# Attention outputs of two heads issued in turn, projections one step ahead and outputs one step behind, in a two-block transformer kernel

## The chip, the cores and the metric

The kernel runs on one core of a Trainium2 chip. The metric is the device time of one execution in microseconds (us), the median of several runs. The profile is one further execution, recorded instruction by instruction.

## The reference, cut to what matters

256 tokens of width 1024 pass through two blocks. The first mixes differential attention, an RWKV recurrence and attention over a memory, and ends in a mixture of 16 experts. The second holds four feed-forward layers, with a mixer after the first (`hybrid_ab_mixer`) and one after the third (`swa_sink_mixer`). What the change touches are the three attentions with heads of 64 columns:

```python
# memory attention: 4 heads of 64
s = jnp.einsum('bshd,bmhd->bhsm', q, mk) * (MEM_HEAD_DIM ** -0.5)
o = jnp.einsum('bhsm,bmhd->bshd', jax.nn.softmax(s, axis=-1), mv)
...
# hybrid mixer: heads A (8 of 64) with a banded, dilated causal bias
o_a = dilated_mixture(qa, ka, va, table[:, :A_HEADS])
# heads B (8 of 64): each query keeps the 64 keys with the best index score
sc = jax.nn.relu(jnp.einsum('bqhd,bsd->bqhs', qib, k_idx))
score = jnp.einsum('bqhs,bqh->bqs', sc, wb) * idx_scale
_, idx = lax.top_k(score, topk)                  # topk = 64
o_b = dsa_attention(qb, kb, vb, q_idx, k_idx, w_idx, table[:, A_HEADS:], topk)
...
# sliding-window mixer: 16 heads of 64, 2 key heads, sinks
o, lse = banded_attention(q, k, v, bias, C_WINDOW - 1)
o = o * jax.nn.sigmoid(lse - sinks)[..., None]
```

## The kernel before, in words

All weights stream from memory in 2 MB pieces (`load`, L91, issued by SyncE). Each piece is cut into slices of 128x1024, and each slice into a high part (`wh`, a copy on ScalarE, L99) and a low part (`wl`, a subtraction on VectorE, L100). A product with weights is three TensorE products (`mm3`, L105 to L107). A framework gives every engine its instruction list: it runs a simulated timeline when the kernel is built and at each point takes, of the instructions that it believes to be ready, the one that the code names first. So the code's order is a priority, and the list that results is fixed: on the chip each engine works through it in that order.

The hybrid mixer (`hyb`) and the sliding-window mixer (`swa`) go over 8 steps, each of two heads (128 columns). A step projects q (and k) for its two heads (`projT`, 24 products of 128x128 by 256 columns each), takes them out of PSUM with one VectorE instruction (`evac_rows`, L386), makes the scores (`attn_scores`, L295 and L296 on TensorE, then bias, maximum, exponential and division on VectorE and ScalarE, L301 to L312), transposes the weights (L325), copies them to SBUF (`pT`, L327) and multiplies with v (L329, L330). The last two products exist once for each head `e` of the pair and write 64 partitions of one PSUM bank, `po[64*e:64*e+64]`; they use 64 columns of the array. ScalarE and VectorE take the bank out as a high and a low part (L331, L332). fp32 products appear as two records each in the trace.

`staggered` runs the steps: `first(j+1)` (projection and scores) is named ahead of `second(j)` (transposes, copies and products with v, in `attn_out`); after the last `first` the first part of the output projection (`project_back`) is named. For each head `attn_out` names transposes, copy and both products before it turns to the next head.

In `hyb` the heads B need an additive mask `madd`. `index()`, called at step 2, makes it: 6 small projections, 8 pairs of score products (L492, L494), 16 VectorE instructions that add them up (L500), and then for each of two query blocks 8 rounds of `max` and `match_replace` (L507, L509), which strike out the 64 best keys. Steps 4 to 7 add the mask to their bias on GpSimd (L538).

`mem_attn` in the first block does the same as `attn_out` over two steps with 256 keys (L1095 transposes, L1098 copies, L1101 products). `diff_attn` and the expert layer use `staggered` too, with their own `first` and `second`.

Of the kernel before, what the change touches and what calls it, by code (L numbers as in the profile page):

```python
# [11 lines left out]
F32 = mybir.dt.float32  # L12
# [4 lines left out]
OP = mybir.AluOpType  # L17
# [4 lines left out]
T = 256  # L22
# [4 lines left out]
class Net:  # L27
# [364 lines left out]
    def swa(self, h, x, follow):  # L392
        W = self.I["swa"]
        xh, xl, rs = x
        kv = self.projN(self.by_k(self.load(self.I["swa_kv"]), 256), 0, 256, xh, xl, True)
        v = self.natural([ps[:, 128:] for ps in kv], self.pair(128, "vs0", "vs1"), rs)
        kT = [self.repeated_T([ps[:, 64 * g:64 * g + 64] for ps in kv], rs, "kT", 2) for g in range(2)]
        bc = self.row_bc(rs)
        oh, ol = self.o_tiles()
        raws, bias = {}, {}  # L400

        def first(j):
            g, c = divmod(j, 4)
            if j % 2 == 0:
                bias[0] = self.load_bias(16 + 2 * j)
            if c == 0:
                raws[g] = self.load(W[g])
            qT = self.evac_rows(self.projT(self.by_col(raws[g], c), xh, xl), bc, 0.125, "qT", 2)
            return self.attn_scores(qT, kT[g], [self.head_bias(bias[0], 2 * (j % 2) + e) for e in range(2)],
                                    self.col("sinks", 2 * j, 2))  # L410

        x, after = follow()
        self.staggered(8, first, lambda j, s2: self.attn_out(s2, v, [64 * (j // 4)] * 2, oh, ol, j),
                       self.project_back([W[2], W[3]], oh, ol, h, range(8), TAIL["swa"], after))
        return x

    def natural(self, ps, out, rs):
# [21 lines left out]
    def hyb(self, h, x, follow):  # L439
        nc, wk = self.nc, self.ph  # L440
        W = self.I["hyb"]
# [31 lines left out]
        def index():  # L473
# [14 lines left out]
            for hd in range(8):  # L488
# [10 lines left out]
                for b, sl, cz in blocks:  # L499
                    nc.vector.scalar_tensor_tensor(new[:, sl], rl[:, sl], cw[b][:, 256 + hd:257 + hd],  # L500
                                                   cz if score is None else score[:, sl], OP.mult, OP.add)
                score = new
            for b, sl, _ in blocks:
                cur = score
                for it in range(8):
                    m8 = wk.tile([128, 8], F32, name=self.nm("m8"), tag="m8", bufs=2)
                    nc.vector.max(m8, cur[:, sl])  # L507
                    nxt = wk.tile([128, 384], F32, name=self.nm("rep"), tag="score", bufs=3)
                    nc.vector.match_replace(nxt[:, sl], m8, cur[:, sl], -3.0e38)  # L509
                    cur = nxt  # L510
                nc.vector.tensor_scalar(madd[:, sl], cur[:, sl], -2.0e38, -1.0e30, OP.is_gt, OP.mult)

        oh, ol = self.o_tiles()
        raws, bias = {}, {}

        def first(j):
# [4 lines left out]
            c = 2 * (j % 2)  # L521
            hb = [self.head_bias(bias[0], c + e) for e in range(2)]
            if j < 4:
                if j % 2 == 0:
                    raws[0] = self.load(W[1 + j // 2])
                qT = self.evac_rows(self.projT(self.by_col(raws[0], c), xh, xl), bc, 0.125, "qa", 2)
                kT = self.evac_rows(self.projT(self.by_col(raws[0], c + 1), xh, xl), bc, 1.0, "ka", 2)
                return self.attn_scores(qT, kT, hb)
# [4 lines left out]
            kT = self.evac_rows(self.projT(self.by_col(raws[0], j - 4), xh, xl), bc, 1.0, "ka", 2)  # L533
# [6 lines left out]
            return self.attn_scores(qb[j - 4], kT, bb)  # L540

        def second(j, s2):
            c = 128 * (j % 4)
            self.attn_out(s2, v[j // 4], [c, c + 64], oh, ol, j)

        x, after = follow()
        self.staggered(8, first, second,
                       self.project_back([W[5], W[6]], oh, ol, h, range(8), TAIL["hyb"], after))
        return x

    def mixers(self, x, more, follow):
# [512 lines left out]
    def mem_attn(self, qT, kT, mkv, oh, ol):  # L1064
# [22 lines left out]

        def second(j, s2):
            po = self.acc()
            for e in range(2):  # L1090
                r = slice(64 * e, 64 * e + 64)
# [5 lines left out]
                pT = sb([512], "mpT", 2)  # L1097
                nc.scalar.copy(pT, pt)  # L1098
                c = 256 + 128 * j + 64 * e
                for kb in range(2):  # L1100
                    nc.tensor.matmul(po[r, :T], mkv[kb][:, c:c + 64], pT[:, kb * 256:kb * 256 + 256],  # L1101
                                     start=kb == 0, stop=kb == 1)
# [591 lines left out]
```

## Time and profile before

| what | before |
|---|---|
| runs | 1427.21, 1427.64, 1431.28 us; median 1427.64 |
| profiled execution | 1430.63 us, its span 1428.9 us |
| TensorE clock granted, mean over the span | 0.979 |
| TensorE products busy | 1378.0 us (96%) |
| VectorE busy | 747.7 us (52%) |
| ScalarE busy | 610.0 us (43%) |
| HBM read | 291.45 MB |

The span runs from the first to the last instruction of the profiled execution; the rest of its own time, 1.7 us, lies around it. Busy times of TensorE are modelled, and overlapping records are counted once, so distances from one start to the next say more than durations. In the views PE is TensorE, PEld its weight loads, DVE VectorE, ACT ScalarE, POOL GpSimd, SP SyncE. Times are us from the start of the span.

### The profile page before, as it was taken

How to read it: one execution, taken by the hardware profiler on the slowest of the kernel's cores; microseconds unless marked ns; L12 is line 12 of the kernel's file. 1: busy time of each engine (PE TensorE's matmuls, PEld its weight loads, DVE VectorE, ACT ScalarE, POOL GpSimd, SP SyncE). 2: the span in 40 equal slices, each digit the busy share in tenths (PEclk: the TensorE clock that was granted, in tenths of full speed). 3: DMA queues.
4: the chain of work that ended last, by engine and by line, in shares of the span. 5: the costliest groups of instructions: out<-in, count | busy, mean ns of one | idle time of the engine just before them, and what ended most of it. 6: DMA issues, size and time to landing. Idle time of an engine off the chain costs nothing.

```text
span 1428.9 us, 18895 instructions
## 1 busy us (share of the span) xinstructions
PE 1378.0 (96%) x7650; PEld 1051.2 (74%) x7650; DVE 747.7 (52%) x1250; ACT 610.0 (43%) x961; POOL 77.5 (5%) x123
## 2 busy tenths in 40 slices
PE   8999989998998999999999999999999989999997
PEld 7787664343336888888777888878888877788886
DVE  6867641121116655457865655455554567555543
ACT  5545421011113544347454544345444366545442
POOL 1133100000000000000110000000000000000001
PEclk9999889999998999999999999999999999999999
DMA  7262489999956555446334555445553642464420
GB/s 315 93 230 91 185 327 414 409 424 428 422 216 236 183 191 184 153 171 251 115 106 147 184 191 183 178 178 188 189 205 125 241 158 75 139 229 177 177 89 30
DMA packets 35370, 293.81 MB, mean 206 GB/s; under 512 B 3728, under 2 KB 8112, under 8 KB 16080
## 3 DMA queue, kind: packets, MB, share of 16 engines
q1 hardware_dynamic: 29952, 286.58, 53.1%
q10 hardware_dynamic: 5328, 5.98, 1.3%
q8 instruction: 62, 1.02, 0.3%
q14 instruction: 28, 0.23, 0.0%
HBM read 291.45 MB, written 1.10 MB: 205 GB/s over the span
## 4 chain that ended last, share of the span: by engine, by line
PE 65%; DVE 3%; ACT 1%; issue 1%; ACTq 0%; POOLq 0%; POOL 0%
PE acc L105 20%; PE acc L107 20%; PE acc L106 20%; PE tr L213 1%; PE acc L329 1%; DVE wl L100 1%; PE tr L325 1%; PE acc L296 1%; PE acc L295 1%; PE acc L330 0%; ACT sq L119 0%; DVE h L376 0%; DVE h L378 0%; DVE xf L139 0%; ACT wh L99 0%
## 5 line engine op out<-in xcount | busy, mean ns | idle before, releaser
L100 DVE TENSOR_TENSOR wl<-raw,wh 128x1024 fp32r<-128x1024 f32 (+1 forms) x349 | 426.1, 1224 | 377.0 <-ACT wh L99 374.9
L99 ACT CAST wh<-raw 128x1024 fp32r<-128x1024 f32 (+1 forms) x349 | 364.6, 1048 | 408.6 <-PE acc L107 358.1
L105 PE MATMUL acc<-wh,xh 128*128 128x512 f32 (+1 forms) x896 | 334.5, 375 | 2.4 <-ACT xh L140 1.8
L107 PE MATMUL acc<-wh,xl 128*128 128x512 f32 (+2 forms) x896 | 333.2, 373 | 1.7 <-DVE xl L141 1.5
L106 PE MATMUL acc<-wl,xh 128*128 128x512 f32 (+1 forms) x896 | 333.1, 372 | 0.0
L105 PEld LDWEIGHTS acc<-wh,xh 128*128 128x128 f32 x896 | 170.4, 190 | 32.2 <-ACT xh L140 3.0
L107 PEld LDWEIGHTS acc<-wh,xl 128*128 128x128 f32 x896 | 170.3, 190 | 31.7 <-DVE xl L141 3.7
L106 PEld LDWEIGHTS acc<-wl,xh 128*128 128x128 f32 x896 | 170.5, 190 | 28.3 <-DVE lent L732 0.6
L107 PE MATMUL acc<-wh,hl 128*128 128x512 f32 x352 | 137.5, 391 | 0.0
L106 PE MATMUL acc<-wl,hh 128*128 128x512 f32 x352 | 137.1, 389 | 0.0
L105 PE MATMUL acc<-wh,hh 128*128 128x512 f32 x352 | 137.0, 389 | 0.0
L106 PEld LDWEIGHTS acc<-wl,hh 128*128 128x128 f32 x352 | 66.1, 188 | 13.8
L105 PEld LDWEIGHTS acc<-wh,hh 128*128 128x128 f32 x352 | 66.1, 188 | 13.5
L107 PEld LDWEIGHTS acc<-wh,hl 128*128 128x128 f32 x352 | 66.1, 188 | 13.4
L105 PE MATMUL acc<-xh,wh 128*128 128x256 f32 x224 | 67.6, 302 | 1.2 <-ACT wh L99 0.6
L106 PE MATMUL acc<-xl,wh 128*128 128x256 f32 x224 | 65.6, 293 | 0.6 <-DVE xl L141 0.6
L107 PE MATMUL acc<-xh,wl 128*128 128x256 f32 x224 | 65.7, 295 | 0.0
L111 POOL TENSOR_SCALAR rstd<-ss 128x1 f32<-128x1 f32 x22 | 9.3, 422 | 965.8 <-ACT sq L119 964.3
L1303 PE MATMUL acc<-half,xe 128*64 128x512 f32 x248 | 59.6, 596 | 0.0
L1336 DVE TENSOR_SCALAR yf<-tr,gate 128x512 f32<-128x512 f32 x16 | 12.0, 751 | 81.0 <-PE tr L1329 80.8
L105 PEld LDWEIGHTS acc<-xh,wh 128*128 128x128 f32 x224 | 45.2, 202 | 5.0 <-issue 2.4
L106 PEld LDWEIGHTS acc<-xl,wh 128*128 128x128 f32 x224 | 45.1, 201 | 1.1 <-DVE xl L141 0.9
(454 smaller groups left out, 1681.5 us busy)
## 6 DMA issues: line engine op xcount, KB each, us to landing
raw<-in_ffn SPq DMA_DIRECT2D x63, 2048.0 KB, 8.0
half<-in_moe SPq DMA_DIRECT2D x45, 1024.0 KB, 12.9
raw<-in_moe SPq DMA_DIRECT2D x13, 2048.0 KB, 16.0
raw<-in_hyb SPq DMA_DIRECT2D x7, 2048.0 KB, 8.2
wl<-in_moe SPq DMA_DIRECT2D x23, 512.0 KB, 13.4
wh<-in_moe SPq DMA_DIRECT2D x23, 512.0 KB, 14.4
raw<-in_win SPq DMA_DIRECT2D x4, 2048.0 KB, 10.7
raw<-in_swa SPq DMA_DIRECT2D x4, 2048.0 KB, 9.2
```

What stands on the lines that cost most here:

```text
L99: nc.scalar.copy(hi[:, :n], x)
L100: nc.vector.tensor_tensor(lo[:, :n], x, hi[:, :n].bitcast(F32), OP.subtract)
L105: mm(out, a[0], b[0], start=start, stop=False)
L106: mm(out, a[0], b[1], start=False, stop=False)
L107: mm(out, a[1], b[0], start=False, stop=stop)
L213: nc.tensor.transpose(ps[:, i * 128:(i + 1) * 128], m[:, i * 128:(i + 1) * 128], self.ident)
L295: nc.tensor.matmul(ps[:, 0:128], qT[r, 0:128], kT[r, 0:128], start=True, stop=True)
L296: nc.tensor.matmul(ps[:, 128:384], qT[r, 128:256], kT[r, :], start=True, stop=True)
L325: nc.tensor.transpose(pt[:, i * 128:(i + 1) * 128], s2[e][:, i * 128:(i + 1) * 128], self.ident)
L329: nc.tensor.matmul(po[r, :T], v[0][:, c:c + 64], pT[:, :T], start=True, stop=False)
L1303: last = mm(ps[c][e * 64:e * 64 + 64, :], xe[:, k, o + e * 64:o + e * 64 + 64], w[i][e][:, c * 512:c * 512 + 512], start=k == 0, stop=k == 7)
L1336: nc.vector.tensor_scalar(yf, po[a], gate[:, 0:1], None, OP.mult)
```

## The change

Four edits. (1) The products with v of the two heads of a pair are issued in turn: first key block of head 0, of head 1, then the second key block of head 0, of head 1. The first of the four waits for the copy of the second head (`wait_for`), so that all four are ready at once. This is done in `attn_out` (hyb and swa) and in `mem_attn`. (2) `attn_out` becomes a generator: transposes and copies first, the products one step later. (3) The projections of a step move out of `first` into `prepare`, which runs one step further ahead; the buffers of q, k and `pT` get one, one and two more. (4) `index()` becomes a generator in three parts, called in `prepare(1)`, `prepare(2)` and `prepare(3)`, and its rounds go over both query blocks in turn instead of one block after the other.

```diff
     def attn_out(self, s2, v, vcol, oh, ol, j):
         nc, wk = self.nc, self.ph
-        po = self.acc()
+        pT = []
         for e in range(2):
-            r = slice(64 * e, 64 * e + 64)
             pt = self.trp()
...
-            pT = wk.tile([128, 384], F32, name=self.nm("pT"), tag="pT", bufs=2)
-            nc.scalar.copy(pT, pt[:, :384])
-            c = vcol[e]
-            nc.tensor.matmul(po[r, :T], v[0][:, c:c + 64], pT[:, :T], start=True, stop=False)
-            nc.tensor.matmul(po[r, 128:T], v[1][:, c:c + 64], pT[:, T:], start=False, stop=True)
+            pT.append(wk.tile([128, 384], F32, name=self.nm("pT"), tag="pT", bufs=4))
+            last = nc.scalar.copy(pT[e], pt[:, :384])
+        yield
+        po = self.acc()
+        for kb, q, z in ((0, slice(0, T), slice(0, T)), (1, slice(128, T), slice(T, 384))):
+            for e in range(2):
+                c = vcol[e]
+                m = nc.tensor.matmul(po[64 * e:64 * e + 64, q], v[kb][:, c:c + 64], pT[e][:, z], start=kb == 0,
+                                     stop=kb == 1)
+                if kb == e == 0:
+                    self.wait_for(m, last)
...
-    def staggered(self, n, first, second, then=()):
+    def staggered(self, n, first, second, then=(), prepare=lambda j: None):
+        for j in range(min(n, 2)):
+            prepare(j)
         kept = first(0)
         then = iter(then)
+        rest = iter(())
         for j in range(n):
-            ahead = first(j + 1) if j + 1 < n else next(then, None)
-            second(j, kept)
+            ahead = first(j + 1) if j + 1 < n else None
+            for _ in rest:
+                pass
+            if j + 1 == n:
+                next(then, None)
+            rest = second(j, kept) or iter(())
+            next(rest, None)
             kept = ahead
-        for _ in then:
+            if j + 2 < n:
+                prepare(j + 2)
+        for _ in itertools.chain(rest, then):
             pass
...
# hyb, index(): after the score sums
+            yield
+            for it in range(8):
+                nxt = wk.tile([128, 384], F32, name=self.nm("rep"), tag="score", bufs=3)
+                for b, sl, _ in blocks:
+                    m8 = wk.tile([128, 8], F32, name=self.nm("m8"), tag="m8", bufs=2)
+                    nc.vector.max(m8, score[:, sl])
+                    nc.vector.match_replace(nxt[:, sl], m8, score[:, sl], -3.0e38)
+                score = nxt
+                if it == 3:
+                    yield
...
+        def prepare(j):
+            if 0 < j < 4:
+                next(steps)
             if j % 2 == 0:
-                bias[0] = self.load_bias(2 * j)
-            if j == 2:
-                index()
+                bias[j] = bias[j + 1] = self.load_bias(2 * j)
...
# mem_attn, second(): the copies of both heads first, then
+            for kb in range(2):
+                for e in range(2):
+                    c = 256 + 128 * j + 64 * e
+                    m = nc.tensor.matmul(po[64 * e:64 * e + 64, :T], mkv[kb][:, c:c + 64],
+                                         pT[e][:, kb * 256:kb * 256 + 256], start=kb == 0, stop=kb == 1)
+                    if kb == e == 0:
+                        self.wait_for(m, last)
```

`swa` gets a `prepare` of the same kind (bias, weights, `projT` and `evac_rows`), and its `first(j)` only calls `attn_scores`.

## Rows read from the trace of the kernel before

**Rows 1.** The page: busy time of each engine.
```profile
PE 1378.0 (96%) x7650; PEld 1051.2 (74%) x7650; DVE 747.7 (52%) x1250; ACT 610.0 (43%) x961; POOL 77.5 (5%) x123
```
**Rows 2.** Timeline of TensorE, a swa step: start, length, line, operation, records merged.
```profile
1175.76 0.28 PE L105 MATMUL acc<-xh,wh 128*128 128x256 f32 x1
1175.88 0.28 PE L106 MATMUL acc<-xl,wh 128*128 128x256 f32 x1
1176.09 0.65 PE L329 MATMUL acc<-pT,vs 128*64 128x256 f32 x2
1176.57 0.38 PE L330 MATMUL acc<-pT,vs 128*64 128x128 f32 x2
1176.88 0.39 PE L107 MATMUL acc<-xh,wl 128*128 128x256 f32 x1
1177.10 0.28 PE L105 MATMUL acc<-xh,wh 128*128 128x256 f32 x1
```
**Rows 3.** Timeline of TensorE where both heads stand together, end of hyb and swa.
```profile
751.76 0.66 PE L329 MATMUL acc<-pT,ch 128*64 128x256 f32 x4
752.24 0.40 PE L330 MATMUL acc<-pT,cl 128*64 128x128 f32 x4
752.57 0.50 PE L107 MATMUL acc<-wh,ol 128*128 128x512 f32 x1
...
1227.11 0.66 PE L329 MATMUL acc<-pT,vs 128*64 128x256 f32 x4
```
**Rows 4.** Timeline of TensorE in the memory attention.
```profile
165.56 1.08 PE L1101 MATMUL acc<-mpT,mkv 128*64 128x256 f32 x4
166.57 0.66 PE L1095 MATMUL tr<-ident,ms 128*128 128x128 f32 x4
```
**Rows 5.** Busy time by stretch: length, PE, PEld, DVE, ACT, POOL, PEclk, DMA share, GB/s.
```profile
1173.80:1205.50 31.70, 31.70 (x232) 25.25 (x231) 24.04 (x96) 21.89 (x71) 0.00 (x0) 1.00 0.34 118
716.55:735.59 19.04, 19.04 (x141) 15.17 (x139) 14.87 (x52) 12.18 (x37) 5.75 (x10) 1.00 0.32 111
653.14:715.69 62.55, 58.83 (x414) 50.50 (x412) 49.77 (x154) 36.13 (x78) 5.37 (x6) 0.95 0.51 185
675.00:714.00 39.00, 35.80 (x232) 29.73 (x231) 33.84 (x110) 20.11 (x42) 5.37 (x6) 0.91 0.35 119
687.30:693.40 6.10, 6.08 (x30) 4.75 (x31) 5.45 (x27) 2.24 (x9) 0.00 (x0) 0.50 0.60 183
1161.00:1164.40 3.40, 3.40 (x19) 2.83 (x16) 2.18 (x13) 2.24 (x10) 0.00 (x0) 0.51 0.00 0
...
220.00:380.00 160.00, 155.29 (x740) 64.88 (x737) 26.49 (x50) 21.64 (x40) 0.00 (x0) 1.00 1.01 421
```
**Rows 6.** Timeline of TensorE in hyb, step 2: the wait, and both heads together.
```profile
687.32 0.81 PE L295 MATMUL acc<-ka,qa 64*128 64x128 f32 x4 [3.20 <-DVE ka L386]
...
688.91 1.13 PE L329 MATMUL acc<-pT,va 128*64 128x256 f32 x4
```
**Rows 7.** Groups of VectorE instructions, 675 to 716 us: count, busy, mean ns, idle.
```profile
L500 DVE SCALAR_TENSOR_TENSOR score<-rl,cw,score 128x256 f32<-128x256 f32 x7 | 3.3, 478 | 0.0
L507 DVE MAX8 m<-rep 128x8 f32<-128x256 f32 x7 | 3.0, 424 | 0.1
L509 DVE MATCH_REPLACE8 rep<-m,rep 128x256 f32<-128x256 f32 x7 | 2.9, 408 | 0.0
L500 DVE SCALAR_TENSOR_TENSOR score<-rl,cw,score 128x128 f32<-128x128 f32 x7 | 2.4, 346 | 0.0
L507 DVE MAX8 m<-rep 128x8 f32<-128x128 f32 x7 | 2.0, 286 | 0.0
L509 DVE MATCH_REPLACE8 rep<-m,rep 128x128 f32<-128x128 f32 x7 | 1.9, 275 | 0.0
...
L509 DVE MATCH_VALUE_LOAD rep<-m,rep 128x8 f32 x14 | 1.2, 86 | 0.2
```
**Rows 8.** Timeline of VectorE where the third weights' low part and `ka` stand.
```profile
685.04 1.22 DVE L100 TENSOR_TENSOR wl<-raw,wh 128x1024 fp32r<-128x1024 f32 x1
...
686.76 0.42 DVE L386 SCALAR_TENSOR_TENSOR ka<-acc,bc 128x256 f32<-128x256 f32 x1
```
**Rows 9.** Timeline of VectorE and TensorE at the start of swa's steps.
```profile
1157.78 2.35 DVE L100 TENSOR_TENSOR wl<-raw,wh 128x1024 fp32r<-128x1024 f32 x2
...
1160.52 0.50 PE L295 MATMUL acc<-kT,qT 64*128 64x128 f32 x4 [1.39 <-DVE qT L386]
```

More of the change, by code (lines that the diff above doesn't have):

```diff
@@ L399, in swa, with first @@
         oh, ol = self.o_tiles()
-        raws, bias = {}, {}
-        def first(j):
+        raws, bias, qT = {}, {}, {}
+        def prepare(j):
             g, c = divmod(j, 4)
             if j % 2 == 0:
-                bias[0] = self.load_bias(16 + 2 * j)
+                bias[j] = bias[j + 1] = self.load_bias(16 + 2 * j)
             if c == 0:
                 raws[g] = self.load(W[g])
-            qT = self.evac_rows(self.projT(self.by_col(raws[g], c), xh, xl), bc, 0.125, "qT", 2)
-            return self.attn_scores(qT, kT[g], [self.head_bias(bias[0], 2 * (j % 2) + e) for e in range(2)],
+            qT[j] = self.evac_rows(self.projT(self.by_col(raws[g], c), xh, xl), bc, 0.125, "qT", 3)
+        def first(j):
+            return self.attn_scores(qT[j], kT[j // 4], [self.head_bias(bias[j], 2 * (j % 2) + e) for e in range(2)],
                                     self.col("sinks", 2 * j, 2))
@@ L413, in swa @@
         self.staggered(8, first, lambda j, s2: self.attn_out(s2, v, [64 * (j // 4)] * 2, oh, ol, j),
-                       self.project_back([W[2], W[3]], oh, ol, h, range(8), TAIL["swa"], after))
+                       self.project_back([W[2], W[3]], oh, ol, h, range(8), TAIL["swa"], after), prepare)
         return x
@@ L502, in index @@
                 score = new
-            for b, sl, _ in blocks:
[L504 to L511, printed above, removed]
@@ L513, in hyb @@
-        oh, ol = self.o_tiles()
-        raws, bias = {}, {}
-        def first(j):
-            if j % 2 == 0:
-                bias[0] = self.load_bias(2 * j)
-            if j == 2:
-                index()
-            c = 2 * (j % 2)
-            hb = [self.head_bias(bias[0], c + e) for e in range(2)]
+            yield
[8 more added lines that the diff above has]
+                    yield
@@ L523, in first, with prepare @@
+            for b, sl, _ in blocks:
+                nc.vector.tensor_scalar(madd[:, sl], score[:, sl], -2.0e38, -1.0e30, OP.is_gt, OP.mult)
+            yield
+        oh, ol = self.o_tiles()
+        raws, bias, qT, kT = {}, {}, {}, {}
+        steps = index()
+        def prepare(j):
+            if 0 < j < 4:
+                next(steps)
+            if j % 2 == 0:
+                bias[j] = bias[j + 1] = self.load_bias(2 * j)
             if j < 4:
+                c = 2 * (j % 2)
                 if j % 2 == 0:
@@ L525, in first @@
                     raws[0] = self.load(W[1 + j // 2])
-                qT = self.evac_rows(self.projT(self.by_col(raws[0], c), xh, xl), bc, 0.125, "qa", 2)
-                kT = self.evac_rows(self.projT(self.by_col(raws[0], c + 1), xh, xl), bc, 1.0, "ka", 2)
-                return self.attn_scores(qT, kT, hb)
+                qT[j] = self.evac_rows(self.projT(self.by_col(raws[0], c), xh, xl), bc, 0.125, "qa", 3)
+                kT[j] = self.evac_rows(self.projT(self.by_col(raws[0], c + 1), xh, xl), bc, 1.0, "ka", 3)
@@ L529, in first @@
+                return
             if j == 4:
@@ L532, in first @@
                 raws[0] = self.load(W[4])
-            kT = self.evac_rows(self.projT(self.by_col(raws[0], j - 4), xh, xl), bc, 1.0, "ka", 2)
+            kT[j] = self.evac_rows(self.projT(self.by_col(raws[0], j - 4), xh, xl), bc, 1.0, "ka", 3)
+        def first(j):
+            hb = [self.head_bias(bias[j], 2 * (j % 2) + e) for e in range(2)]
+            if j < 4:
+                return self.attn_scores(qT[j], kT[j], hb)
             bb = []
@@ L539, in first @@
                 bb.append((t[:, :128], t[:, 128:]))
-            return self.attn_scores(qb[j - 4], kT, bb)
+            return self.attn_scores(qb[j - 4], kT[j], bb)
         def second(j, s2):
             c = 128 * (j % 4)
-            self.attn_out(s2, v[j // 4], [c, c + 64], oh, ol, j)
+            return self.attn_out(s2, v[j // 4], [c, c + 64], oh, ol, j)
         x, after = follow()
         self.staggered(8, first, second,
-                       self.project_back([W[5], W[6]], oh, ol, h, range(8), TAIL["hyb"], after))
+                       self.project_back([W[5], W[6]], oh, ol, h, range(8), TAIL["hyb"], after), prepare)
         return x
@@ L1089, in second @@
             po = self.acc()
+            pT = []
             for e in range(2):
-                r = slice(64 * e, 64 * e + 64)
                 pt = self.trp()
@@ L1096, in second @@
                                             s2[e][:, t * 256 + kb * 128:t * 256 + kb * 128 + 128], self.ident)
[L1097 to L1102, printed above, removed]
+                pT.append(sb([512], "mpT", 2))
+                last = nc.scalar.copy(pT[e], pt)
+            for kb in range(2):
[5 more added lines that the diff above has]
+                        self.wait_for(m, last)
             nc.scalar.copy(oh[:, 6 + j, :], po[:, :T])
```

4 lines of the change are left out of this document (added).

## The prediction

> **What bounds the kernel now.** I read the page first: TensorE is busy for 1378.0 us, 96% of the span, VectorE for about half [rows 1]. Any TensorE time taken away is therefore worth itself, as long as nothing else in the same stage is nearly as busy. So the second view is busy time by stretch, for the stages that the change touches [rows 5]. In swa's steady steps (five in 31.70 us, 6.34 us each) TensorE never stands, VectorE is busy for 24.04 and ScalarE for 21.89 us. In hyb's steps with heads B (three in 19.04 us, 6.35 each) the picture is the same, VectorE 14.87. In the first half of hyb, 653.14 to 715.69, it is not: VectorE is busy for 49.77 of 62.55 us, for 33.84 of 39 us between 675 and 714, and TensorE waits. The third view, TensorE's timeline, shows where: 3.20 us before the scores of step 2, on the evacuation of `ka` [rows 6], and 1.39 us before swa's first scores, on `qT` [rows 9]. The granted clock is at half (0.50, 0.51: 1.2 of 2.4 GHz) for 6.1 us behind the first wait and 3.4 us behind the second [rows 5].
>
> **Part 1: two heads in turn (the main term).** In swa the second head's products stand alone between projection products [rows 2]. Projection products follow each other at 0.12 us (1175.76, 1175.88). With the block between them it takes 1177.10 - 1175.88 = 1.22 us for what would be two such distances, so the block costs 1.22 - 0.24 = 0.98 us: 0.79 from its start to the next product, and 0.1 lost on either side. What the pair costs when it stands together needs no guess, since it does so three times already: beside the scores of hyb's step 2 (outputs of step 1) [rows 6] and at the last steps of both mixers, x4 records of L329 in a row [rows 3]. At full clock both heads then take 752.57 - 751.76 = 0.81 us, as good as one head alone. So wherever the heads are apart, joining them saves 0.98 - 0.02 = 0.96 us. In the timelines 13 of the 16 steps have them apart (steps 0 to 6 of swa; 0 and 2, and 3 to 6, of hyb): 13 x 0.96 = 12.5 us.
>
> The new wait: the first of four products waits for the second head's copy, and as TensorE works in order, everything behind it waits too. But the products are also named a whole step after the copies, over 5 us later, so in hyb and swa I cost it at nothing; without that delay it would cost a copy per step. In the memory attention there is no such delay, but there are products of the output projection to fill with. There a head costs 166.57 - 165.56 = 1.01 us [rows 4] and about 0.14 for the two sides (estimated by the 0.1 above); two steps give 2 x 1.15 = 2.3 us. The expert layer that follows runs with the DMA engines at 1.01 of their time [rows 5], and could give this back by waiting for weights; TensorE is busy for 155.29 of 160 us there, so I take 2.3 and keep 0 as lower end.
>
> **Part 2: the index spread over steps, hyb's first half.** The sums, rounds and masks stay the same in number: 16 sums, and per round a maximum, a value load and a replacement for each block [rows 7]. They start one step earlier (in `prepare(1)`, not at step 2), and q and k are evacuated a step before they are needed, so the evacuation that was late, `ka` behind a 1.22 us weight subtraction and index rounds [rows 8], has a step's slack. What can be won: the wait of 3.20 us, and (1 - 0.50) x 6.1 = 3.0 us of half clock, 6.2 in all. But VectorE has the same 49.77 us to do in this stretch, and less time. Its share in the dense part was 33.84/39 = 0.868; at that share it needs 49.77/0.868 = 57.3 us, which is 5.2 less than now. Of these 5.2, 2 x 0.96 = 1.9 are part 1's two steps, so 3.3 us remain. I take 3.3, between 0 (another wait takes its place) and 6.2.
>
> **Part 3: projections ahead in swa.** The low parts of the weights of steps 1 and 2 are made from 1157.78 on for 2.35 us, so the first is there at about 1158.96 [rows 9]; TensorE could do step 1's projection while it waits for `qT`, but has the scores ahead of it in its list. With `prepare(1)` named ahead of `first(0)` it does. Worth the 1.39 us, and with it up to (1 - 0.51) x 3.4 = 1.7 us of half clock. I take the wait and half of the clock, 2.2 us, between 0 and 3.1.
>
> **Part 4: what gets tighter.** A swa step shrinks to 6.34 - 0.96 = 5.38 us, and VectorE's 24.04/5 = 4.81 us fill 0.89 of it; in hyb's steps 14.87/3 = 4.96 us fill 0.92 of 5.39. At the share of 0.868 the steps would be 5.54 and 5.71 us, 0.16 and 0.32 more; over 7 and 4 steps 2.4 us. That share is the highest over a long stretch here, but no limit that a row shows, so I take half, -1.2 us, between 0 and -2.4.
>
> The Trainium skill speaks against the change at this point: "TensorEngine Tiling (Array Packing)", section PSUM Bottleneck, says that tiling speeds up TensorE but not the emptying of PSUM, which may then become the bottleneck. The rows show both emptying engines below TensorE even in the shortened step, so by the rows part 1 stays; by the rule most of it would go, which is the first rival below.
>
> Moved without cost: eight bias loads, issued from ScalarE's queue, come a step earlier; the weight loads on SyncE's queue keep their order. What hides them is that each buffer named ahead has been free for a step.
>
> **The sum.** 12.5 + 2.3 + 3.3 + 2.2 - 1.2 = 19.1 us. The profiled execution took 1430.63 us (span 1428.9), so it would take 1411.5; the median of the runs is 3.0 us lower, 1427.64, and 1427.64 - 19.1 = **1408.5 us**. With every upper end, 12.5 + 2.3 + 6.2 + 3.1 = 24.1, it is 1403.5; with every lower end, 12.5 - 2.4 = 10.1, it is 1417.5. Less than 0.3%, 4.3 us, can hardly be told from no change.
>
> **Rivals.**
> - *VectorE becomes the bound of the steps.* If it can't be busier than in swa's steady steps now, 24.04/31.70 = 0.76, eleven steps don't shrink and hyb's first half gains nothing beyond part 1; left are 2 x 0.96 + 2.3 + 2.2 = 6.4 us: 1421.2. For it: 0.89 and 0.92 is a lot for an engine whose instructions depend on each other. Against it: 0.868 over 39 us is there already. Chance 0.08.
> - *The pairs don't stay together, or hardly.* The list is made from simulated times, and transposes or scores that become ready between the four products may be put between them. If six of the 13 break, 6 x 0.96 = 5.8 us go, and with parts 2 and 3 at nothing 1427.64 - (12.5 - 5.8 + 2.3 - 1.2) = 1419.8. Against it: four products that become ready at one time and stand together in the code. Chance 0.04.
> - *No change.* TensorE's time is saved but something else sets the end, such as the weights of the next layer: 1427.6. Against it: DMA engines at 0.34 and 0.32 in these steps [rows 5]. Chance 0.05.
> - *Slower: the rounds come as bursts.* Before, one block's rounds were a chain, and other work slipped in between [rows 8]. Two chains in turn leave no such gaps: four rounds of both blocks are 4 x (0.424 + 0.408 + 0.286 + 0.275 + 2 x 0.086) = 6.3 us without a break, twice, and the 16 sums 16 x 0.41 = 6.6 us [rows 7]. If each of the three bursts stops TensorE for 6.3 us and is followed by the 3.0 us of half clock that the wait in rows 6 brought, that is 27.9 us, against 12.5 + 2.3 + 2.2 - 1.2 + 6.2 = 22.0 (the old wait gone): 5.9 us slower, 1433.5. It turns slower from 22.0/3 - 3.0 = 4.3 us a burst. Against it: q and k are a step ahead. Chance 0.05.
>
> **Numbers.** The forecast has 0.78, the rivals 0.08, 0.04, 0.05 and 0.05. Faster: 0.78 + 0.08 + 0.04 = 0.90; the same 0.05; slower 0.05. The range takes the forecast's own ends, 1403.5 and 1417.5, and reaches to the second rival's 1419.8: 1403 to 1420.
>
> **What would show it.** Part 1: records of L329's and L330's successors in rows of four, 16 times, 0.81 us each, and swa steps of some 5.4 us. Part 2: no wait of TensorE above 1 us between the first scores of hyb and step 4's, and no half clock there. Part 3: step 1's projection ahead of swa's first scores. Part 4: VectorE at about 0.9 in the steady steps. The prediction is wrong if TensorE gets new waits on VectorE's evacuations or on `madd`, or if the pairs are apart.

## The result, and the profile after

The changed kernel takes 1414.97 us (median; 1413.60 to 1416.25) where the kernel before takes 1427.43 beside it (1426.86 to 1431.28): a ratio of 0.9907, interval 0.9890 to 0.9924, 12.5 us less. The forecast was 1408.5 us, in a range of 1403 to 1420: faster as predicted, but by 12.5 us and not by 19.1. The profiled execution of the changed kernel took 1414.69 us, its span 1413.0. One more execution of the changed kernel, in the last series, took 1540.57 us at a granted clock of 0.842 over its span and is left out of every comparison.

The page of the changed kernel, busy time of each engine:

```profile
PE 1357.5 (96%) x7650; PEld 1040.7 (74%) x7650; DVE 744.6 (53%) x1250; ACT 609.3 (43%) x961; POOL 75.0 (5%) x123
```

TensorE's work is 20.5 us less than in [rows 1] and its share is the same, so it still sets the end. TensorE's timeline of the changed kernel, a swa step (start, length, line, operation, records merged):

```profile
1171.89 0.50 PE L295 MATMUL acc<-kT,qT 64*128 64x128 f32 x4
1172.22 0.61 PE L296 MATMUL acc<-kT,qT 64*128 64x256 f32 x4
1172.76 0.87 PE L333 MATMUL acc<-pT,vs 128*64 128x256 f32 x8
1173.56 0.39 PE L105 MATMUL acc<-xh,wh 128*128 128x256 f32 x1
1173.78 0.28 PE L106 MATMUL acc<-xl,wh 128*128 128x256 f32 x1
1173.90 0.27 PE L107 MATMUL acc<-xh,wl 128*128 128x256 f32 x1
...
1176.52 1.15 PE L325 MATMUL tr<-ident,sc 128*128 128x128 f32 x6
1177.59 0.50 PE L295 MATMUL acc<-kT,qT 64*128 64x128 f32 x4
```

Eight records in a row, both heads, 0.80 us from their start to the next product: what one head alone took in [rows 2]. All 16 pairs of hyb and swa stand in such rows. But a step is not 5.38 us: from 1161.57 to 1189.68 there are five, 5.62 us each (5.32 to 5.87).

The waits of parts 2 and 3 have not gone. TensorE's timeline of the changed kernel at step 1 of hyb, and at the start of swa's steps; the bracket is the wait and who ended it:

```profile
671.05 0.61 PE L296 MATMUL acc<-ka,qa 64*128 64x256 f32 x4
674.37 0.81 PE L295 MATMUL acc<-ka,qa 64*128 64x128 f32 x4 [2.71 <-DVE ka L409]
...
1150.72 0.40 PE L248 MATMUL tr<-ident,rstd 128*128 128x128 f32 x2
1153.31 0.50 PE L295 MATMUL acc<-kT,qT 64*128 64x128 f32 x4 [2.19 <-DVE qT L409]
```

VectorE's timeline of the changed kernel at the same two places:

```profile
664.21 0.74 DVE L525 SCALAR_TENSOR_TENSOR score<-rl,cw,causal 128x128 f32<-128x128 f32 x2
664.87 4.69 DVE L525 SCALAR_TENSOR_TENSOR score<-rl,cw,score 128x128 f32<-128x128 f32 x14
...
672.17 1.21 DVE L100 TENSOR_TENSOR wl<-raw,wh 128x1024 fp32r<-128x1024 f32 x1
673.30 0.60 DVE L533 MAX8 m<-rep 128x8 f32<-128x128 f32 x2
673.83 0.40 DVE L409 SCALAR_TENSOR_TENSOR ka<-acc,bc 128x256 f32<-128x256 f32 x1
...
1151.70 1.23 DVE L100 TENSOR_TENSOR wl<-raw,wh 128x1024 fp32r<-128x1024 f32 x1 [0.42 <-ACT wh L99]
1152.84 0.75 DVE L409 SCALAR_TENSOR_TENSOR qT<-acc,bc 128x256 f32<-128x256 f32 x2
```

In hyb the wait of [rows 6] (3.20 us, step 2) has become one of 2.71 us at step 1: the sums and the first rounds now start a step earlier, so the `ka` that stands behind them, and behind a weight subtraction, is a step earlier too. Two more of 0.74 and 0.38 us follow in steps 2 and 3. In swa both projections are done by 1150.7, as part 3 said, but the wait is 2.19 us where [rows 9] has 1.39: the two `qT` stand behind a weight subtraction that starts when their second factor `bc` is still being made (transposed at 1150.72).

Busy time by stretch of the changed kernel (length, then busy us of the engines, granted clock, DMA share, GB/s): hyb's first half, four swa steps, and the stretch at half clock behind the wait in hyb:

```profile
651.00:709.92 58.92, 54.66 (x405) 48.55 (x404) 47.45 (x152) 36.17 (x77) 4.39 (x6) 0.97 0.53 198
1166.89:1189.68 22.79, 22.66 (x190) 18.64 (x188) 19.26 (x77) 17.61 (x57) 0.00 (x0) 1.00 0.34 117
674.20:677.60 3.40, 3.23 (x15) 2.61 (x16) 3.40 (x17) 2.42 (x6) 0.00 (x0) 0.50 0.02 5
```

The forecast's terms, put together by place, against the two profiled executions (distances between the same instructions):

| place | forecast | measured | how |
|---|---|---|---|
| memory attention | 2.3 | 1.6 | 45.0 to 43.4 us, first scores to the transposes of the layer behind it |
| hyb, to the scores of step 4 | 2 x 0.96 + 3.3 = 5.2 | 3.8 | 87.3 to 83.5; 3.4 us less at half clock, worth 1.7 of it |
| hyb, from there | 4 x 0.96 - 0.64 = 3.2 | 2.9 | 45.4 to 42.5 |
| swa | 7 x 0.96 + 2.2 - 0.56 = 8.4 | 6.1 | 90.4 to 84.3; 3.4 us less at half clock |
| sum | 19.1 | 14.4 | of 15.9 us by the spans |

The other 1.5 us lie in layers that the change doesn't touch; in the expert layer, from 192 us on, the execution of after has 10.2 us at half clock and that of before 13.7. The swa line is one execution's: in a second one of the changed kernel (the last experiment) swa took 82.3 us, and the other three places the same to 0.1. By the medians it is 12.5, not 15.9: the profiled execution of before took 3.2 us more than its median, that of after 0.3 less.

### The profile page after: what moved, and what is told of

Same layout as the page of the kernel before. It is cut to its first block, busy times and chain, and to the rows that moved or that the text cites. A ratio compares the mean times of both kernels' runs of the same rounds, so it can differ in the third digit from the quotient of the medians.

```text
span 1413.0 us, 18913 instructions
## 1 busy us (share of the span) xinstructions
PE 1357.5 (96%) x7650; PEld 1040.7 (74%) x7650; DVE 744.6 (53%) x1250; ACT 609.3 (43%) x961; POOL 75.0 (5%) x123
## 4 chain that ended last, share of the span: by engine, by line
PE 62%; DVE 4%; ACT 1%; issue 1%; ACTq 0%; POOLq 0%; POOL 0%
PE acc L105 20%; PE acc L107 20%; PE acc L106 19%; PE tr L213 1%; DVE wl L100 1%; PE acc L333 1%; PE tr L325 1%; ACT wh L99 1%; PE acc L295 0%; DVE rep L534 0%; PE acc L296 0%; ACT sq L119 0%; DVE h L401 0%; DVE h L399 0%; DVE xf L139 0%
## 5 line engine op out<-in xcount | busy, mean ns | idle before, releaser
L106 PEld LDWEIGHTS acc<-wl,hh 128*128 128x128 f32 x352 | 66.1, 188 | 13.7
## 6 DMA issues: line engine op xcount, KB each, us to landing
raw<-in_moe SPq DMA_DIRECT2D x13, 2048.0 KB, 14.5
wh<-in_moe SPq DMA_DIRECT2D x23, 512.0 KB, 14.5
raw<-in_win SPq DMA_DIRECT2D x4, 2048.0 KB, 10.2
```

The source lines that it names most:

```text
L106: mm(out, a[0], b[1], start=False, stop=False)
```

## Experiments

Each run is compared with the kernel before in the same series (1427.58 to 1428.85 us).

### Pairs alone

The kernel before, with the four products adjacent and nothing else:

```diff
+            pT.append(wk.tile([128, 384], F32, name=self.nm("pT"), tag="pT", bufs=2))
+            last = nc.scalar.copy(pT[e], pt[:, :384])
+        po = self.acc()
+        for kb, q, z in ((0, slice(0, T), slice(0, T)), (1, slice(128, T), slice(T, 384))):
+            for e in range(2):
...
+                if kb == e == 0:
+                    self.wait_for(m, last)
```

> The kernel before with the four 64-column products of two heads adjacent (in attention and in memory attention) and nothing else: no output one step behind, no projection one step ahead, index rounds as before, two buffers of transposed probabilities. Theory A (two heads computed at the same time are the gain, and the rest of the change moves waits without removing them): the 13 pairs that stood apart fall from 1.6 to 0.8 us each, 10 to 12 us, and memory attention about 2, and TensorE then waits for the second head's copy in front of the products only where nothing else is queued: 10 to 14 us under the kernel before, within 3 us of the changed kernel. Rival B (the output one step behind is needed: without it TensorE stands in front of the products until ScalarE has copied the second head's probabilities, some 0.5 us in each of 16 steps, which the trace of memory attention shows as 0.46 us): 8 us are given back, and it is only 4 to 6 us under the kernel before.

1419.21 us, ratio 0.9933 (0.9915 to 0.9952): 9.4 us less, three quarters of the changed kernel's gain; theory A asked for 10 to 14. TensorE's timeline of this kernel, hyb's step 2 and a swa step:

```profile
684.00 0.81 PE L295 MATMUL acc<-ka,qa 64*128 64x128 f32 x4 [3.54 <-DVE ka L396]
...
1169.58 0.87 PE L331 MATMUL acc<-pT,vs 128*64 128x256 f32 x8 [0.17 <-ACT pT L326]
```

Steps of 5.71 us, 0.63 less than before, with a wait for the second copy of 0.2 us. So the rest of the change, products named a step behind and projections ahead, is worth some 0.1 us a step in swa, not the half microsecond of rival B: swa as a whole takes 84.4 us here and 84.3 (82.3 in a second execution) in the changed kernel. The reason is in TensorE's list. The framework's simulated timeline had already put the projection of a later step ahead of the transposes: in both kernels a step reads scores, products with v, projection, transposes, next scores. The largest difference between this kernel and the changed one is in hyb's first half: 86.1 us against 83.5.

### Order inside the four products

```diff
-        for kb, q, z in ((0, slice(0, T), slice(0, T)), (1, slice(128, T), slice(T, 384))):
-            for e in range(2):
+        for e in range(2):
+            for kb, q, z in ((0, slice(0, T), slice(0, T)), (1, slice(128, T), slice(T, 384))):
```

> The changed kernel with the four products of a pair in the order head 0 twice, then head 1 twice, still adjacent and still behind the second copy. Theory A (adjacency on TensorE is what lets the two column halves run at the same time; the last steps of the kernel before stood in this order and a pair took 0.8 us): within 2 us of the changed kernel. Rival C (the products must alternate between the halves, one half after the other otherwise): each of 16 pairs takes some 0.7 to 0.8 us more, so 11 to 13 us over the changed kernel, near the kernel before.

1415.32 us, ratio 0.9904 (0.9888 to 0.9921), the same as the changed kernel's. TensorE's timeline of this kernel, the pair in a swa step:

```profile
1172.98 0.88 PE L333 MATMUL acc<-pT,vs 128*64 128x256 f32 x8
1173.79 0.39 PE L105 MATMUL acc<-xh,wh 128*128 128x256 f32 x1
```

0.81 us. "In turn" does not matter; adjacent does. Rival C falls.

### Heads apart, the rest of the change kept

Head 1's two products are named behind the next projection, in memory attention behind its own copy:

```diff
+            if e == 0:
+                yield
...
-            for _ in rest:
-                pass
+            next(rest, None)
...
+            behind = rest
...
+            for _ in behind:
+                pass
```

> The changed kernel with its projections ahead, its outputs one step behind and its spread rounds, but with head 1's two products queued behind the projection of the step after, so that the two heads are apart in 14 of 16 steps, and memory attention's heads one after the other as in the kernel before. Theory A (the pairs are nearly the whole gain): 14 x 0.8 to 0.96 plus about 2 for memory attention, so 12 to 16 us over the changed kernel, and so within 3 us of the kernel before. Rival D (ahead, behind and spread rounds carry a good part of the gain by themselves): it stays 5 us or more under the kernel before.

1423.90 us, ratio 0.9963 (0.9951 to 0.9976): 4.8 us less than before, 9 more than the changed kernel. TensorE's timeline of this kernel, one head on either side of transposes and scores:

```profile
1179.05 0.86 PE L333 MATMUL acc<-pT,vs 128*64 128x256 f32 x4
1179.85 0.87 PE L325 MATMUL tr<-ident,sc 128*128 128x128 f32 x6
...
1181.51 0.86 PE L333 MATMUL acc<-pT,vs 128*64 128x256 f32 x4
1182.31 0.38 PE L105 MATMUL acc<-xh,wh 128*128 128x256 f32 x1
```

0.80 us for each head, steps of 6.32 us. Pairs alone give 9.4, everything but pairs 4.8, both together 12 to 13: nearly a sum. Theory A's 12 to 16 us was too high, and rival D's 5 us just missed.

### Where the index work stands

Three variants of the changed kernel's hyb. First, the copies `qa` and `ka` named ahead of the index work of their step:

```diff
-            if 0 < j < 4:
-                next(steps)
...
+                if j:
+                    next(steps)
```

> The changed kernel with the parts of the index work (score sums, rounds of max and replace) named behind the projections and their two copies out of PSUM instead of ahead of them in the hybrid stage. Theory A (the 2.71 us wait of step 1's scores and the half clock that follows it come from the copy ka standing behind the index sums on VectorE): the wait shrinks to under 0.5 us, 2 to 4 us under the changed kernel. Rival E (VectorE is the bound of that half of the stage, so whatever is pulled ahead makes something else late: the additive masks of step 4, or the maxima of the softmax): the wait at step 1 goes and one of about the same size comes up to the scores of step 4, and the time stays within 1 us of the changed kernel.

1418.48 us, ratio 0.9924 (0.9904 to 0.9945): no gain, the median 3.5 us over the changed kernel's. TensorE's timeline of this kernel, the waits in hyb's first half:

```profile
681.82 0.70 PE L325 MATMUL tr<-ident,sc 128*128 128x128 f32 x3 [2.41 <-DVE sc L312]
...
690.04 0.50 PE L295 MATMUL acc<-ka,qa 64*128 64x128 f32 x4 [1.16 <-DVE ka L409]
...
699.51 0.50 PE L295 MATMUL acc<-ka,qa 64*128 64x128 f32 x4 [1.13 <-DVE ka L409]
```

The wait at the scores of step 1 is gone and the division of the softmax is late instead, and `ka` in steps 2 and 3: 4.7 us of waits in place of 3.8. That is rival E in kind, though it looked for the new wait at step 4 and for no more than 1 us over. Second, all the index work in one piece ahead of step 2:

```diff
-            if 0 < j < 4:
-                next(steps)
+            if j == 2:
+                for _ in steps:
+                    pass
```

> The changed kernel with all the index work (sums, eight rounds, mask) in one piece ahead of step 2's projections, outputs one step behind and projections one ahead as they are. Theory A (spreading the rounds buys nothing, since VectorE is full in that stretch either way): within 1.5 us of the changed kernel, the wait at step 1's scores replaced by one of 2 to 4 us at step 2's. Rival H (the spread is what the two-head pairs alone lack, and gives the 3 to 4 us between the kernel with only the pairs and the changed one): 3 to 4 us over the changed kernel, at the time of the kernel with only the pairs.

1417.12 us, ratio 0.9928 (0.9915 to 0.9942), some 2 us over the changed kernel, the intervals overlapping: between the theories. TensorE's timeline of this kernel has the wait of the kernel before again:

```profile
685.62 0.89 PE L295 MATMUL acc<-ka,qa 64*128 64x128 f32 x4 [3.77 <-DVE ka L409]
```

It is followed by 6.8 us at half clock, against 3.4 in the changed kernel; hyb's first half takes 86.3 us, like the pairs alone (86.1). So the spread of the index can account for the 2.8 us in that half, but 1.7 of them are clock (3.4 us fewer at half), and that is not sure to come with it: the run with the other order inside the four products has the changed kernel's index work and waits (2.72, 0.74, 0.32 us), but 6.8 us at half clock, and the half takes 84.9 us. Busy time by stretch of that run, behind the wait of 2.72 us:

```profile
673.20:680.00 6.80, 6.38 (x30) 5.76 (x31) 6.04 (x32) 4.41 (x15) 0.00 (x0) 0.50 0.01 2
```

Third, the index cut later, in four parts:

```diff
-            yield
+                if hd % 4 == 3:
+                    yield
...
+                if j:
+                    next(steps)
...
+            if j == 4:
+                next(steps)
```

> The changed kernel with the index work of the hybrid stage cut later and in four parts instead of three: eight of the score sums behind the projections of step 1, eight behind those of step 2, four rounds behind those of step 3, and four rounds with the mask ahead of those of step 4, where VectorE stood idle 5.7 us of ten in the changed kernel. Theory E (between the first sum and step 3's division VectorE has no idle time at all, so a wait there goes only when work leaves that stretch): the waits ahead of scores in hybrid steps 1 to 3 (2.71, 0.38 us) and the half clock fall away, 2 to 5 us under the changed kernel. Rival G (VectorE isn't the limit but the order inside it, and another order only makes something else late, as naming the copies first did): a wait of 2 us or more comes up elsewhere in the half, and the time is within 1 us of the changed kernel or over it.

1415.32 us, ratio 0.9915 (0.9899 to 0.9931), no gain: rival G. In TensorE's timeline of this kernel the waits are 3.50 us in sum:

```profile
675.87 0.70 PE L325 MATMUL tr<-ident,sc 128*128 128x128 f32 x3 [1.40 <-DVE sc L312]
...
692.10 0.81 PE L295 MATMUL acc<-ka,qa 64*128 64x128 f32 x4 [2.10 <-DVE ka L409]
```

### The row of norms first

In swa `bc`, the factor that `qT` waits for, is named ahead of the repeated keys:

```diff
-        kT = [self.repeated_T([ps[:, 64 * g:64 * g + 64] for ps in kv], rs, "kT", 2) for g in range(2)]
         bc = self.row_bc(rs)
+        kT = [self.repeated_T([ps[:, 64 * g:64 * g + 64] for ps in kv], rs, "kT", 2) for g in range(2)]
```

> The changed kernel with the row of reciprocal norms that the queries are multiplied by (its transpose on TensorE and its copy on ScalarE) named ahead of the repeated keys in the sliding-window stage. In the changed kernel both projections are done by 1150.7 us and the first scores stand 2.19 us behind qT, whose multiplication had no second factor before 1151.6. Theory A (that late factor is the wait): the wait falls to under 0.7 us and the time is 1 to 2.5 us under the changed kernel. Rival F (qT is late because it stands behind a 1.2 us split of weights on VectorE, or the repeated keys become the late ones): a wait of 1.3 us or more stays, and the time is within 0.7 us of the changed kernel.

1413.05 us, ratio 0.9900 (0.9885 to 0.9915), the interval overlapping the changed kernel's. TensorE's timeline of this kernel at swa's first scores:

```profile
1151.65 0.27 PE L457 MATMUL tr<-ident,cn 128*128 128x128 f32 x1
1151.95 0.50 PE L295 MATMUL acc<-kT,qT 64*128 64x128 f32 x4
```

The wait of 2.19 us is gone (one of 0.68 comes up later, ahead of transposes), and swa takes 81.6 us instead of 84.3. The late factor was the wait; 2.7 us less in the stage, 2 by the medians; but a second execution of the changed kernel took 82.3 us for the stage, so the size is less sure than the cause. Both edits together:

> The later cut of the index work and the earlier row of norms together, on the changed kernel. Theory: the two are in different stages and add up: the sum of the two runs beside it, 3 to 7 us under the changed kernel by the expectations of those, some 1408 to 1412 us. Rival: the first makes a wait or a half-clock stretch in the second stage and the sum is under half of that.

1412.10 us, ratio 0.9901 (0.9886 to 0.9916), just outside the 1408 to 1412 that was expected; the later cut had gained nothing by itself, so there was little to add up. The profiled execution took 1409.40, with no half clock in hyb at all, though the wait of 2.10 us before `ka` is there as in the run with the later cut alone. Busy time by stretch, 3.4 us from about the end of that wait, of the kernel with the later cut and then of the one with both edits:

```profile
692.00:695.40 3.40, 3.30 (x17) 1.94 (x18) 3.40 (x17) 0.61 (x3) 0.00 (x0) 0.50 0.00 0
```

```profile
690.60:694.00 3.40, 3.40 (x24) 2.45 (x25) 3.40 (x16) 1.17 (x6) 0.00 (x0) 1.00 0.00 0
```

The same wait in the same order of hyb's instructions, once with half clock behind it and once without.

### What holds a step at 5.6 us

On top of both edits, the division of the softmax on GpSimd, for both heads and then for the second alone:

```diff
-                    nc.vector.tensor_scalar(s[:, sl], s[:, sl], den[:, b:b + 1], None, OP.mult)
+                    nc.gpsimd.tensor_scalar(s[:, sl], s[:, sl], den[:, b:b + 1], None, OP.mult)
```

> The kernel with the later index and the earlier norms, with the division of the softmax (four instructions of 0.2 to 0.3 us a step) on GpSimd, which does nothing in the sliding-window steps, in place of VectorE. Theory J (VectorE's queue holds the steps at some 5.65 us instead of the 5.38 that TensorE's work adds up to, since the evacuation of the next queries stands behind the softmax of the step before): 0.9 us a step less on VectorE, steps of 5.4 to 5.5 us, 2 to 4 us under the kernel without it. Rival K (it is the length of the chain from scores to transposes, not the fullness of VectorE: GpSimd took 0.60 and 0.86 us for a 128x128 and a 128x256 addition, so each head's division becomes about 1 us longer): transposes wait 0.5 us or more a step, 3 us or more over the kernel without it.

> The same with the division of the second head alone on GpSimd. Theory J: steps of 5.5 us, 1 to 2.5 us under the kernel without it, and under the run with both if there the chain is too long. Rival K: the second head's transposes come last in a step anyway, and are late by the 1 us that its division takes longer: no gain, or 1 to 3 us over.

1422.50 us (0.9952, 0.9936 to 0.9969) and 1422.87 (0.9958, 0.9942 to 0.9974), 10 us more than without. Busy time by stretch of the kernel with both divisions on GpSimd, four swa steps:

```profile
1169.79:1192.79 23.00, 21.83 (x184) 17.94 (x182) 15.36 (x61) 16.93 (x56) 11.48 (x16) 1.00 0.33 116
```

VectorE is busy for 0.67 of the time instead of 0.85, and the steps are 5.75 us, no shorter; at the end of the steps TensorE waits once more, for 2.35 us. Theory J falls: with a fifth of its work gone from VectorE the steps are no shorter. But the divisions are also slower on GpSimd (0.60 and 0.92 us for a head's two, where VectorE takes 0.55 for both), so these runs lengthen the chain from scores to transposes as they unload VectorE; alone they show that this chain matters, not that VectorE's load doesn't. Rival K has the direction; the 1 to 3 us that it gave for the second head alone were 10.8. VectorE's timeline of the changed kernel, the step shown at the top, has the chain, which closes once a step:

```profile
1172.15 1.23 DVE L100 TENSOR_TENSOR wl<-raw,wh 128x1024 fp32r<-128x1024 f32 x1 [0.35 <-ACT wh L99]
1173.29 0.28 DVE L301 CUSTOM_DVE_ANT_0 sc<-acc,bias 128x128 f32<-128x128 f32 x1
...
1176.62 0.55 DVE L312 TENSOR_SCALAR sc<-sc,den 128x128 f32<-128x128 f32 x2
1177.08 0.42 DVE L409 SCALAR_TENSOR_TENSOR qT<-acc,bc 128x256 f32<-128x256 f32 x1
```

Scores from 1171.89, bias and maximum from 1173.29 (a weight subtraction stands ahead of them), the second head's division from 1176.62, then the queries of the next step from 1177.08, and next scores at 1177.59. The transposes between take 1.07 us here, 0.84 to 1.12 in four steps, where the kernel before took 0.75: that is where the steps lose their time, though TensorE's busy share hardly shows it. The last test moves the transposes a real step behind: they must come behind the projection of two steps on.

```diff
+                if i == 0:
+                    self.wait_for(m, self.projected)
...
+            if j + 2 < n:
+                prepare(j + 2)
             for _ in rest:
                 pass
```

> The kernel with the later index and the earlier norms, with the transposes of a step really one step behind its scores on TensorE's list: each is made to come behind the projection of two steps on, so that a step reads scores, projection, products, transposes of the step before. In the list of the changed kernel, as of the kernel before, the transposes of a step stand ahead of the next step's scores, so the chain from scores through the softmax to the transposes closes once a step. Theory L (that chain holds the steps at 5.6 to 5.7 us, not the fullness of any engine): steps of 5.35 to 5.45 us at TensorE's own work, 13 steps times 0.2 to 0.3, so 2 to 4 us under the kernel without it, the best of all runs, some 1408 to 1410 us. Rival M (another wait holds them: the next queries are only multiplied out of PSUM behind the softmax on VectorE): a wait on qT ahead of the scores of 0.2 us or more a step, no gain.

1413.72 us, ratio 0.9888 (0.9869 to 0.9908). TensorE's timeline of this kernel, a swa step, and busy time by stretch, four steps:

```profile
1172.02 0.28 PE L107 MATMUL acc<-xh,wl 128*128 128x256 f32 x1
1172.22 0.87 PE L335 MATMUL acc<-pT,vs 128*64 128x256 f32 x8
1173.03 0.87 PE L325 MATMUL tr<-ident,sc 128*128 128x128 f32 x6
1173.83 0.50 PE L295 MATMUL acc<-kT,qT 64*128 64x128 f32 x4
...
1174.69 0.39 PE L105 MATMUL acc<-xh,wh 128*128 128x256 f32 x1
...
1188.78 0.61 PE L325 MATMUL tr<-ident,sc 128*128 128x128 f32 x3 [1.22 <-DVE sc L312]
```

```profile
1161.18:1183.27 22.09, 22.09 (x186) 18.30 (x185) 19.10 (x79) 17.89 (x61) 0.00 (x0) 1.00 0.38 133
```

TensorE is never idle in these four steps, 5.52 us each and all alike, with VectorE as busy as in the changed kernel (19.10 of 22.09 us, 0.86): the chain was the hold, as theory L said, and not VectorE's load. But the size was off (5.35 to 5.45 us a step and some 1408 to 1410 us were expected), since the list in this order costs 0.14 us more than 5.38: transposes take 0.80 and a projection 3.05 us, against 0.75 (kernel before) and 2.96 (changed kernel) at their shortest. And what the steps win is lost elsewhere: 1.22 us of wait ahead of swa's last transposes, and in hyb 46.4 us from the scores of step 4 on, against 42.7 with both edits alone. As a whole it is level with the two versions above. These three have the lowest medians, 14.5 to 15.5 us under the kernel before, but no interval sets one of them apart from the changed kernel.

### The changed kernel again

> The changed kernel once more, unchanged, beside the two others. Theory (half-clock stretches come and go between executions with the same list of instructions): the median within 1.5 us of 1415, single runs spread over 3 us or more, and a profile whose stretches at half clock differ from the first one's in number by at least one while the waits of the hybrid and the sliding-window stage (2.71 and 2.19 us) are the same to 0.05. Rival: the same waits bring the same half-clock stretches, in the same places.

Ratio 0.9905 (0.9886 to 0.9924), five executions from 1412.56 to 1416.64 us. The waits are there again, 2.71 us in hyb and 2.18 in swa. Busy time by stretch, around the start of swa, of the first profiled execution and of this one:

```profile
1138.40:1141.80 3.40, 3.40 (x19) 3.40 (x18) 1.98 (x4) 1.37 (x3) 0.00 (x0) 0.50 0.81 332
1151.80:1155.20 3.40, 1.89 (x18) 1.51 (x19) 2.72 (x10) 2.01 (x5) 0.00 (x0) 1.00 0.49 92
```

```profile
1138.00:1141.40 3.40, 3.40 (x31) 3.40 (x30) 1.49 (x3) 1.81 (x5) 0.00 (x0) 1.00 0.91 386
1151.80:1155.20 3.40, 3.40 (x19) 2.75 (x17) 2.88 (x19) 2.82 (x13) 0.00 (x0) 0.51 0.79 299
```

One stretch at half clock in each, but in another place. So the rival is out for swa; in hyb, the stretch behind the wait of 2.71 us was there both times. The theory asked for another number of stretches; there were seven in both, so that part of it missed.

## Why the prediction was right, and where it was too high

**Part 1, the mechanism right, the size too high.** All 16 pairs stand together at 0.80 us. The 0.96 us a pair is what the pair itself saves: the blocks of a step at their shortest, pair 0.80, projection 2.96, transposes 0.75 and scores 0.87, make 5.38 us, the step that was forecast. But the pairs alone gave 9.4 us where part 1 adds up to 14.8, since the steps came down by 0.63 us only. The memory attention gave 1.9 us with the pairs alone (44.97 to 43.05) and 1.6 in the changed kernel (43.41); its second pair waits 0.46 us for the second head's copy. That without the delay it would cost a copy per step was too much for hyb and swa: 0.2 to 0.3 us a step.

**Part 4, the reason wrong, the size too small.** 0.08 us a step were taken off for swa, with 0.16 as the end; it is 0.24. (For hyb's steps with heads B 0.16 were taken off; they take 5.53 us, as forecast.) VectorE is not at 0.9 but at 0.85, and taking it down to 0.67 by way of GpSimd doesn't help. The steps end on a chain, scores to softmax to transposes and queries to scores, whose length no busy share shows. So the first rival had the right direction and the wrong cause. The Trainium skill, "TensorEngine Tiling (Array Packing)", section PSUM Bottleneck, says that behind a speed-up by tiling, fourfold in its example, the copies out of PSUM may become the bottleneck; here one such copy, `qT`, ends the chain, but VectorE, which makes it, was not the limit by its load: it was as busy, 0.86, in the shorter steps with the transposes a step behind. The same page, section Key Properties, says that changing the tiling mode drains TensorE; no run here singles that out. The second product behind the pair comes 0.22 us after the first and not 0.12, but behind transposes, which use the whole array, it comes after 0.20 (1168.76 and 1168.96 in the changed kernel). What is measured is that 0.14 us a step hang on the order of the blocks.

**Part 2, the mechanism wrong.** "A step's slack" was not there: index work that is named a step earlier puts the `ka` of that step behind it. The waits were 3.20 us and are 3.83. What was won, 1.9 us beyond the two pairs, is almost all clock (3.4 us at half clock in place of 6.8, 1.7 us). Four places of the index work were run with the pairs (the changed kernel's, copies first, in one piece, later), and each had 3.5 to 4.7 us in waits of over 0.3 us: in the changed kernel VectorE has no idle time at all from 661.9 to 696.5 us, so what is moved in there makes something else late. Less wait was seen where TensorE's own order was another: 1.33 us with the heads apart, where it has more to do, and 2.41 with the transposes a step behind. It was also less where work left VectorE: 2.46 us with both divisions on GpSimd and 2.76 with one, against 3.50 with the same index cut. But that half then took 81.1 and 81.6 us, where the kernel with both edits, like these without half clock there, took 81.4; so how much of it VectorE's load costs stays open. Starting the index work before that stretch was not tried.

**Part 3, wrong.** The projection went ahead as forecast, and the scores waited for something that was not looked at, the factor `bc`. The wait grew by 0.8 us and took the place of the old one; moving `bc` removed it.

**The base.** The sum used the profile of an execution that was 3 us over its median and had two stretches at half clock in swa, where each of the two traces of the changed kernel has one. The 1.7 us of half clock in part 3 were of the kind that comes and goes. The 3.0 us of part 2 were less so: 6.8 us at half clock stand behind hyb's wait at step 2 in all three kernels that have it (3.20 us before, 3.54 with the pairs alone, 3.77 with the index in one piece).

**How much was luck.** The time lies in the range by part 1 and by clock. The waits that parts 2 and 3 were to remove are there again in sum, and longer (3.83 and 2.19 us), so what these two terms added to the agreement was not earned by their mechanism.

## What to carry to other kernels

Two half-width products ran at the same time where they were neighbours on TensorE's list (0.80 us for both, as for one alone); look at the list, not at the order in the code, since the planner may have done (or undone) half of the change already. When an early stall is to be removed by naming its producer earlier, follow every operand of the late instruction, and ask what the work that is pulled ahead pushes back on its own engine. A steady step that ends on a chain got no shorter here by moving a link of it to a slower engine; one more step of pipeline took 0.1 us off it, with no gain in the whole time that is clear of the noise.

## What the hardware showed beyond that

Stretches at half clock (3.4 to 13.7 us long) came and went between executions of the same list: 3.4 us at 1138 us in one execution and at 1152 in the next. Two kernels with the same order in hyb had 3.4 us behind a wait of 2.10 us and none. Single times of one kernel spread by 2 to 7 us, so a cost in half clock that is read off one profile is worth less than the wait that it follows.
